# Making the low part of a weight by an accumulating DMA instead of a VectorE subtraction, in a hybrid decoder trunk on one core

## The chip, the cores and the metric

The program runs on one core of one Trainium2 chip. The metric is the device time of one execution in microseconds (us); the time of a kernel is the median of its runs.

## The reference

Two layers on x (512 tokens, width 1024, float32), then a final RMSNorm. Each layer mixes tokens, then channels:

```
h = rms_norm(x, norm1_w[l]) * (1 + sc1) + sh1
(z, xbc, dt_raw, sb_q, sb_k, sb_v, ds_q, ds_k, ds_v,
 ix_q, ix_k, ix_w, gate_logits) = split(h @ w_in[l])
y_ssd = ssd_mixer(z, xbc, dt_raw, ...)
y_sb  = stick_breaking_attention(sb_q, sb_k, sb_v)
y_dsa = dsa_attention(rope(ds_q), rope(ds_k), ds_v, rope(ix_q), rope(ix_k), ix_w)
merged = g_ssd*(y_ssd @ w_br_ssd[l]) + g_sb*(y_sb @ w_br_sb[l]) + g_dsa*(y_dsa @ w_br_dsa[l])
x = x + g1 * (merged @ w_out[l])
h2 = rms_norm(x, norm2_w[l]) * (1 + sc2) + sh2
x = x + g2 * (square(relu(h2 @ w_up[l])) @ w_down[l])
```

The sh, sc and g vectors come from `silu(c) @ ada_w[l]`; the gates are sigmoids of gate_logits. The weights are float32 and the result has to keep nearly float32 accuracy.

## The kernel before, in words

**How a float32 product is made.** TensorE is fed float32r, which keeps fewer bits than float32. Every weight W is therefore split into H, which is W rounded to float32r, and L = W - H; activations are split likewise. `mm3` (lines 222 to 225) makes one product of three matmuls: weight H by activation H (L223), weight H by activation L (L224), weight L by activation H (L225). A matmul has 512 columns, one for each token.

**Pieces of weights.** A `Job` is one 256-column group of a projection with its accumulation in PSUM. A job of 8 row blocks has two `Piece`s of 4 row blocks, 128x1024 float32 or 512 KB each; a job of 4 row blocks has one. For each piece `emit_split` (lines 509 to 536) issues the load of `raw` on SyncE's queue (L521), a cast of `raw` to `wH` on ScalarE (L533), and `wL = raw - wH` on VectorE (L534). `emit_mm` (line 538) then issues 24 matmuls for the piece: 4 row blocks, 2 groups of 128 columns, 3 matmuls each. The planner (`run`, line 580) keeps two pieces split ahead of the matmuls.

**Buffers.** `raw`, `wH` and `wL` come from pool `wp`, declared with two buffers per name. The program is built with automatic buffers, which adds more where memory allows it: a `wL` buffer is reused by the second to sixth piece after it in most places.

**Order.** `layer` (line 709) yields the jobs of the mixers in the order of the table `ORDER`; these are made by `named` (line 1491). Beside the jobs run streams: index scores, top-k by 16 rounds of max and replace on VectorE (L889, L890), stick-breaking attention (`sbatt`, with scans on VectorE at L949 and selects on GpSimd at L940), sparse attention, the SSD scan, and in layer 0 the products with `ada_w`, also on VectorE (L367). A recording layer with priorities then puts the instructions in order on each engine; splits and evacuations have high priority. Each engine works through its own list in order, and waits on semaphores.

**Other places that are spoken of.** `split` (L216, L217) makes the H and L parts of an activation on ScalarE and VectorE; the copies `paS`, `paH` and `paL` move such parts between partitions by DMA on SyncE's queue; `rope` (line 736) multiplies on GpSimd at L742; L978 makes the low part `ysbL` of the stick-breaking result; `rstd_of` (line 442) needs ScalarE's tables for logarithm and exponential, the gates (L1332) the table for tanh; L1379 is the evacuation of a `bssd` job, which needs its result.

Of the kernel before, what the change touches and what calls it, by code (L numbers as in the profile page):

```python
# [12 lines left out]
AF = mybir.ActivationFunctionType  # L13
ALU = mybir.AluOpType
# [43 lines left out]
class Piece:  # L58
# [4 lines left out]
    def __init__(self, job, k0, nk, first, last):  # L63
        self.job, self.k0, self.nk, self.first, self.last = job, k0, nk, first, last
        self.left = 0
        self.H = None
        self.keep = False
# [16 lines left out]
class Job:  # L84


    def __init__(self, name, src, nk, cols, ms, rhs, evac, need=(), kbase=0, dve=1.3, pre=None, halves=False,
                 each=False, step=4):
        self.name, self.src, self.nk, self.cols, self.ms = name, src, nk, cols, ms
        self.rhs, self.evac, self.need, self.pre = rhs, evac, need, pre  # L90
        self.kbase, self.dve, self.halves, self.each, self.step = kbase, dve, halves, each, step
        self.ps = self.fin = None
        self.bank = None
        self.open = self.left = 0

    def pieces(self):
# [78 lines left out]
def tile_trunk(ctx: ExitStack, tc: tile.TileContext, io, out, depth=DEPTH):  # L175
    nc = tc.nc
    act, dve, pool, pe, sync = nc.scalar, nc.vector, nc.gpsimd, nc.tensor, nc.sync
# [16 lines left out]
    def hl():  # L194
        return (pa.tile([P, T], F32R, name="paH", tag="pa"), pa.tile([P, T], F32R, name="paL", tag="pa"))
# [100 lines left out]
    for i, nm, src in ((0, "ada_b", io["ada_b"].rearrange("l (r c) -> (l r) c", c=P)),  # L296
# [5 lines left out]
        n = src.shape[0]  # L302
# [169 lines left out]
    def split_form(p):  # L472
        j = p.job
        src = j.form(p.k0 // 2)
        if p.keep:
            p.H, p.L = ([ap_.tile([P, T], F32R, name=n, tag=n) for _ in range(p.nk)] for n in ("aH", "aL"))
            with tc.high_priority():
                for k in range(p.nk):
                    split(src[:, k * T:(k + 1) * T], p.H[k], p.L[k])
            return  # L480
        H, L = (wp.tile([P, 1024], F32R, name=n, tag=n)[:, :p.nk * T] for n in ("wH", "wL"))
        with tc.high_priority():
            split(src, H, L)
        p.H, p.L = ([X[:, k * T:(k + 1) * T] for k in range(p.nk)] for X in (H, L))
# [24 lines left out]
    def emit_split(p):  # L509
        j = p.job  # L510
        if isinstance(j, Rows):
            split_form(p)
            return
        w = sum(n for _, n in j.cols)
        n = p.nk * w
        raw = wp.tile([P, 1024], F32, name="raw", tag="raw")
        rv = raw[:, :n].rearrange("p (k c) -> p k c", k=p.nk)
        o = 0
        k0 = j.kbase + p.k0
        for c0, m in j.cols:  # L520
            sync.dma_start(rv[:, :, o:o + m], j.src[:, k0:k0 + p.nk, c0:c0 + m])  # L521
            o += m
        if p.keep:
            w *= 2
            parts = [hl() for _ in range(0, n, w)]
        else:
            w = n
            parts = [(wp.tile([P, 1024], F32R, name="wH", tag="wH"), wp.tile([P, 1024], F32R, name="wL", tag="wL"))]
        p.H, p.L = [], []
        with tc.high_priority():  # L530
            for i, (H, L) in enumerate(parts):
                src = raw[:, i * w:(i + 1) * w]
                act.copy(H[:, :w], src)  # L533
                dve.tensor_sub(L[:, :w], src, H[:, :w])  # L534
                p.H += [H[:, k:k + n // p.nk] for k in range(0, w, n // p.nk)]
                p.L += [L[:, k:k + n // p.nk] for k in range(0, w, n // p.nk)]
# [43 lines left out]
    def run(items, ahead=2, step=2):  # L580
# [43 lines left out]
        while True:  # L624
# [38 lines left out]
            if done_k == 0:  # L663
                i = n = 0
                while len(held) < ahead:
                    look(i + 1)
                    us = [q for q in queue if isinstance(q, Unit)]
                    if i >= len(us):
                        break
                    if us[i].p.H is None:  # L670
                        emit_split(us[i].p)
                        held.append(us[i].p)
                        n += 1
                        on_dve(1.03)
                    i += 1
                if n:
                    for f in late:
                        f()
                    del late[:]
# [29 lines left out]
    def layer(l, lys):  # L709
# [781 lines left out]
        def named(n, needs=()):  # L1491
            k, i = n.rstrip("0123456789"), int(n[len(n.rstrip("0123456789")):] or 0)
            j = plain[k](i) if k in plain else kinds[k](i, needs)
            j.dve = DVE_US.get(k, j.dve)
            return j

        yield from add([named(*((n,) if isinstance(n, str) else n)) for n in ORDER if l or n != "iq1"])
        yield from pair(out_job(2), out_job(3))

# [336 lines left out]
```

## Time and profile before

| | |
|---|---|
| median of 3 runs | 1971.56 us (1969.91 to 1973.83) |
| profiled execution, its own time | 1969.26 us |
| span of its profile | 1967.5 us |
| mean granted TensorE clock | 0.997 |
| TensorE busy | 98% of the span |
| VectorE, ScalarE, GpSimd busy | 70%, 46%, 5% |
| DMA queues of SyncE, share of the 16 DMA engines | 43.2% |

Busy time of an engine is a sum over the whole span; a stage with another balance has to be looked at by itself. The mixers run from about 60 to 612 us (layer 0) and from about 1010 to 1612 us (layer 1); the MLPs fill the rest. An idle stretch before an instruction is put down to what released it last.

### The profile page before, as it was taken

To read this page: it belongs to the slowest core of one execution; us is meant where nothing else is said; L and a number is where in the kernel's file an instruction comes from. 1 tells how busy PE (TensorE), PEld (TensorE's weight loads), DVE (VectorE), ACT (ScalarE), POOL (GpSimd) and SP (SyncE) were. 2 spreads that over 40 slices of the span, in tenths; PEclk is the share of its full clock that TensorE was granted. 3 is DMA by queue.
4 is the path that set the end of the run, shared out by engine and by line. 5 is a ranking of instruction groups with operands and counts; after the bars stand their busy time and mean duration, and the time that the engine had idled before them with its cause. 6 is when DMAs were issued, how large, how long until landed. Compare 5 with 4: busy or idle time off the path is not lost.

```text
span 1967.5 us, 26644 instructions
## 1 busy us (share of the span) xinstructions
PE 1931.2 (98%) x9773; PEld 1593.6 (81%) x9773; DVE 1376.7 (70%) x2508; ACT 909.7 (46%) x1625; POOL 93.7 (5%) x135
## 2 busy tenths in 40 slices
PE   8998999999999999999999999999999999999998
PEld 5787777788888988888898787777888899888886
DVE  4899767977856986333477986687576475676874
ACT  4453626723534533242445536276335255554452
POOL 0110210100000000000000101101000000000000
PEclk9999999999999999999999999999999999999999
DMA  8764453562434695223335534324333334134051
GB/s 285 219 178 129 112 150 113 152 196 86 139 113 139 238 370 173 92 91 96 105 100 143 134 89 97 108 87 122 92 107 113 129 108 150 44 128 150 23 203 43
DMA packets 244040, 263.02 MB, mean 134 GB/s; under 512 B 34124, under 2 KB 192132, under 8 KB 243908
## 3 DMA queue, kind: packets, MB, share of 16 engines
q1 hardware_dynamic: 243328, 261.17, 43.2%
q8 instruction: 77, 1.26, 0.3%
q14 instruction: 55, 0.45, 0.1%
q10 hardware_dynamic: 356, 0.14, 0.0%
q0 software_dynamic: 224, 0.00, 0.0%
HBM read 235.43 MB, written 8.52 MB: 124 GB/s over the span
## 4 chain that ended last, share of the span: by engine, by line
PE 87%; DVE 7%; DMA 3%; issue 1%; ACT 1%; POOL 1%; SPq 0%; ACTq 0%; POOLq 0%; DVEq 0%
PE acc L223 22%; PE acc L225 22%; PE acc L224 22%; PE dn L224 3%; PE dn L225 3%; PE dn L223 3%; PE qk L249 2%; DVE wL L534 1%; PE po L1068 1%; DMA araw<-in_ada_w_dram 1%; PE tr L1059 1%; DVE sc L890 1%; DVE m L889 1%; DVE tmp L949 1%; PE po L974 1%
## 5 line engine op out<-in xcount | busy, mean ns | idle before, releaser
L223 PE MATMUL acc<-aH,wH 128*128 128x512 f32 x1544 | 613.0, 397 | 10.4 <-DVE paL L217 5.2
L225 PE MATMUL acc<-aH,wL 128*128 128x512 f32 x1544 | 606.7, 393 | 0.9 <-DVE wL L534 0.9
L224 PE MATMUL acc<-aL,wH 128*128 128x512 f32 x1544 | 606.1, 393 | 0.0
L533 ACT CAST wH<-raw 128x1024 fp32r<-128x1024 f32 (+2 forms) x262 | 266.5, 1023 | 225.9 <-PE acc L224 177.2
L223 PEld LDWEIGHTS acc<-aH,wH 128*128 128x128 f32 x1544 | 291.1, 189 | 72.4 <-DVE paL L217 6.0
L225 PEld LDWEIGHTS acc<-aH,wL 128*128 128x128 f32 x1544 | 290.9, 188 | 62.6 <-DVE wL L534 2.2
L224 PEld LDWEIGHTS acc<-aL,wH 128*128 128x128 f32 x1544 | 291.3, 189 | 57.3 <-issue 0.7
L534 DVE TENSOR_TENSOR wL<-raw,wH 128x1024 fp32r<-128x1024 f32 (+2 forms) x262 | 311.4, 1198 | 22.9 <-ACT wH L533 15.1
L367 DVE SCALAR_TENSOR_TENSOR aacc<-araw,slab,aacc 128x512 f32<-128x512 f32 x140 | 103.8, 749 | 4.5 <-DMA araw<-in_ada_w_dram 3.0
L223 PE MATMUL acc<-uH,wH 128*128 128x512 f32 x224 | 87.7, 392 | 0.0
L225 PE MATMUL acc<-uH,wL 128*128 128x512 f32 x224 | 87.2, 389 | 0.0
L224 PE MATMUL acc<-uL,wH 128*128 128x512 f32 x224 | 87.1, 389 | 0.0
L217 DVE TENSOR_TENSOR uL<-tmp,uH 128x512 fp32r<-128x512 f32 x32 | 22.0, 691 | 70.3 <-ACT uH L216 70.3
L1732 ACT ACTIVATE tmp<-acc 128x512 f32<-128x512 f32 x30 | 17.7, 594 | 111.8 <-PE acc L225 111.8
L224 PE MATMUL dn<-wL,paH 128*128 128x512 f32 x176 | 68.7, 390 | 0.1
L225 PE MATMUL dn<-wH,paL 128*128 128x512 f32 x176 | 68.5, 389 | 0.0
L223 PE MATMUL dn<-wH,paH 128*128 128x512 f32 x176 | 68.1, 389 | 0.0
L949 DVE TENSOR_TENSOR_SCAN tmp<-tmp 128x512 f32<-128x512 f32 (+1 forms) x64 | 52.5, 825 | 20.3 <-ACT tmp L942 20.3
L742 POOL TENSOR_TENSOR tmp<-tmp,slab 128x512 f32<-128x512 f32 (+1 forms) x20 | 31.6, 1578 | 722.1 <-DVE tmp L741 661.0
L1379 DVE SCALAR_TENSOR_TENSOR tmp<-tg,acc 128x512 f32<-128x512 f32 x16 | 11.0, 685 | 67.0 <-PE acc L225 67.0
L217 DVE TENSOR_TENSOR wL<-rd,wH 128x1024 fp32r<-128x1024 f32 x46 | 55.6, 1219 | 2.6 <-ACT wH L216 2.6
L216 ACT CAST wH<-rd 128x1024 fp32r<-128x1024 f32 x46 | 47.0, 1048 | 19.4 <-DVE rd L1652 14.0
(370 smaller groups left out, 3494.7 us busy)
## 6 DMA issues: line engine op xcount, KB each, us to landing
araw<-in_ada_w_dram SPq DMA_DIRECT2D x192, 256.0 KB, 5.3
raw<-in_w_in_dram SPq DMA_DIRECT2D x96, 512.0 KB, 4.0
raw<-in_w_up_dram SPq DMA_DIRECT2D x64, 512.0 KB, 4.9
raw<-in_w_down_dram SPq DMA_DIRECT2D x32, 512.0 KB, 4.7
rd<-in_w_down_dram SPq DMA_DIRECT2D x32, 512.0 KB, 7.0
raw<-in_w_in_dram SPq DMA_DIRECT2D x56, 256.0 KB, 4.3
acb<-acd SPq DMA_DIRECT2D x32, 256.0 KB, 4.7
raw<-in_w_br_ssd_dram SPq DMA_DIRECT2D x16, 512.0 KB, 4.6
```

Source lines behind the costliest of these rows:

```text
L216: act.copy(H, src)
L217: dve.tensor_sub(L, src, H)
L223: pe.matmul(ps, a[0], b[0], start=start, stop=False)
L224: pe.matmul(ps, a[0], b[1], start=False, stop=False)
L225: pe.matmul(ps, a[1], b[0], start=False, stop=stop)
L249: pe.matmul(ps, q[hh][:, cq], k[n][hh][:, ck], start=n == 0, stop=n == 1)
L367: dve.scalar_tensor_tensor(a, raw, cs[:, k:k + 1], a, op0=ALU.mult, op1=ALU.add)
L533: act.copy(H[:, :w], src)
L534: dve.tensor_sub(L[:, :w], src, H[:, :w])
L742: pool.tensor_tensor(out=b[:r], in0=b[:r], in1=sinT[:r], op=ALU.mult)
L889: dve.max(out=m8, in_=sc[tb])
L949: dve.tensor_tensor_scan(out=nv, data0=nv, data1=nv, initial=1.0, op0=ALU.mult, op1=ALU.bypass)
```

## The change

Jobs that `named` makes, which are the mixers' jobs of `ORDER`, are marked `adds`. For their pieces ScalarE makes two casts of `raw`: N = -(raw rounded), written to the buffer `wL`, and H. A DMA issued by GpSimd then adds `raw` to N in place, so that N becomes raw - H. The subtraction on VectorE is gone for these pieces. The first jobs of layer 0 (`iq0`, `misc`, `iq1`), the first pair of layer 1, the last pair of output jobs of each layer and both MLPs are made as before.

```diff
@@ class Job, __init__
+        self.adds = False
@@ emit_split
         p.H, p.L = [], []
+        if j.adds:
+            (H, N), = parts
+            with tc.high_priority():
+                act.activation(N[:, :w], raw[:, :w], AF.Copy, scale=-1.0)
+                act.copy(H[:, :w], raw[:, :w])
+                nc.gpsimd.dma_start(N[:, :w], raw[:, :w], accum_op=ALU.add)
+            p.H = [H[:, k:k + n // p.nk] for k in range(0, w, n // p.nk)]
+            p.L = [N[:, k:k + n // p.nk] for k in range(0, w, n // p.nk)]
+            return
         with tc.high_priority():
             for i, (H, L) in enumerate(parts):
@@ layer, named
             j.dve = DVE_US.get(k, j.dve)
+            j.adds = True
             return j
```

In the built program 166 pieces are changed: 166 VectorE subtractions go, 166 ScalarE instructions and 166 DMAs on GpSimd's queue come. ScalarE gets 16 table loads in place of 12. Of the 166 changed pieces, 77 take the `wL` buffer of the third piece before them, 1 that of the second, the others of the fourth or an earlier one. The line numbers after the change are one higher in the first half of `emit_split` and ten higher behind it; L535 is the cast to H, L534 the cast to N and L536 the DMA.

GpSimd's list, from the last constant it makes to the first of the index scores, where L742 (L752 after the change) is the multiplication of `rope`. Before:

```order
L274 AFFINE_SELECT slab<-slab 128x128
L732 DMA slab<-in_dt_bias_dram 16x1
L742 TENSOR_TENSOR tmp<-tmp,slab 128x512 x2
L742 TENSOR_TENSOR tmp<-tmp,slab 64x512
L742 TENSOR_TENSOR tmp<-tmp,slab 128x512 x2
L867 AFFINE_SELECT sc<-sc 128x128 x3
```

And after the change:

```order
L275 AFFINE_SELECT slab<-slab 128x128
L742 DMA slab<-in_dt_bias_dram 16x1
L752 TENSOR_TENSOR tmp<-tmp,slab 128x512
L536 DMA wL<-raw 128x1024
L752 TENSOR_TENSOR tmp<-tmp,slab 128x512
L536 DMA wL<-raw 128x1024
L752 TENSOR_TENSOR tmp<-tmp,slab 64x512
L536 DMA wL<-raw 128x1024
L752 TENSOR_TENSOR tmp<-tmp,slab 128x512 x2
L536 DMA wL<-raw 128x1024 x3
```

The first three accumulating DMAs stand between the multiplications of `rope`, one behind each.

TensorE's list with its waits, at the first piece of the first changed job, `qk0` of layer 0 (L223 to L225 before are L224 to L226 after). Before:

```order
L223 MATMUL acc<-aH,wH 128x512 [waits DVE_49]
L224 MATMUL acc<-aL,wH 128x512
L776 MATMUL tr<-slab,tmp 128x8 [waits PE_49,Activation_49]
L776 MATMUL tr<-slab,tmp 128x8 x2
L225 MATMUL pb<-aH,wL 128x512 [waits DVE_49]
L225 MATMUL pb<-aH,wL 128x512
...
L225 MATMUL acc<-aH,wL 128x512 [waits DVE_49]
```

And after the change:

```order
L226 MATMUL pb<-aH,wL 128x512
L224 MATMUL acc<-aH,wH 128x512 [waits DVE_49]
L225 MATMUL acc<-aL,wH 128x512
L224 MATMUL acc<-aH,wH 128x512 [waits DVE_49]
L225 MATMUL acc<-aL,wH 128x512
L226 MATMUL acc<-aH,wL 128x512 [waits DMASW7_49]
L226 MATMUL acc<-aH,wL 128x512
L224 MATMUL acc<-aH,wH 128x512
```

The first matmul that reads this `wL` waits for the DMA now, not for VectorE, and the rest of job `iq1` (into `pb`) stands ahead of it instead of between.

ScalarE's list with its waits at the first two changed pieces. Before:

```order
L533 CAST wH<-raw 128x1024 [waits DMAHW6_49,DMAHW7_49,DVE_49,PE_49]
L533 CAST wH<-raw 128x1024 [waits DMAHW1_49,DMAHW2_49,DVE_49,PE_49]
L765 ACTIVATE s_638<-acc,slab 16x512 [waits DMASW5_49,PE_49]
L767 ACTIVATE tmp<-acc 32x512
L745 CAST paH<-tmp 128x512 [waits DVE_49]
```

And after the change:

```order
L535 CAST wH<-raw 128x1024 [waits DMAHW6_49,DMAHW7_49,PE_49,Activation_49]
L534 ACTIVATE wL<-raw 128x1024 [waits PE_49]
L775 ACTIVATE s_638<-acc,slab 16x512 [waits DMASW5_49,PE_49]
L777 ACTIVATE tmp<-acc 32x512
L755 CAST paH<-tmp 128x512 [waits DVE_49]
L534 ACTIVATE wL<-raw 128x1024 [waits DMAHW1_49,DMAHW0_49]
L535 CAST wH<-raw 128x1024 [waits Activation_49]
```

Each piece has two ScalarE instructions now, in either order, one right behind the other.

## Rows read from the trace of the kernel before

**Rows 1.** The page, busy time by engine.
```profile
PE 1931.2 (98%) x9773; PEld 1593.6 (81%) x9773; DVE 1376.7 (70%) x2508; ACT 909.7 (46%) x1625; POOL 93.7 (5%) x135
```

**Rows 2.** Busy time by stretch: its us, engines with instructions, clock, DMA share, GB/s.
```profile
75.00:200.00 125.00, 118.34 (x557) 95.42 (x558) 121.54 (x275) 62.04 (x109) 10.11 (x19) 0.99 0.60 165
...
400.00:500.00 100.00, 100.00 (x513) 82.94 (x512) 73.08 (x108) 35.24 (x50) 0.68 (x1) 1.00 0.43 135
...
1080.00:1200.00 120.00, 115.77 (x561) 93.50 (x560) 107.69 (x246) 59.20 (x100) 14.46 (x28) 0.99 0.42 107
```

**Rows 3.** TensorE's own waits: us in total, times, longest.
```profile
PE acc L223 <- DVE paL L217: 5.2, 1, 5.2
PE qk L249 <- DMA paH<-paL: 4.5, 5, 1.9
...
PE acc L223 <- DVE ysbL L978: 4.0, 1, 4.0
...
PE acc L225 <- DVE wL L534: 0.9, 2, 0.5
```

**Rows 4.** Stretches right behind the two longest of these waits.
```profile
168.80:172.00 3.20, 3.11 (x7) 2.48 (x8) 3.20 (x9) 0.00 (x0) 0.00 (x0) 0.50 0.55 125
...
1130.70:1134.00 3.30, 3.25 (x9) 2.61 (x10) 3.30 (x5) 0.00 (x0) 0.00 (x0) 0.60 0.05 16
```

**Rows 5.** Busy time of line 534 alone, by stretch: VectorE, clock, DMA share, GB/s.
```profile
1080.00:1131.00 51.00, 7.29 (x6) 1.00 0.49 129
75.00:168.80 93.80, 14.63 (x13) 1.00 0.66 181
```

**Rows 6.** Groups of instructions by line and form: busy us, mean ns, idle before.
```profile
L534 DVE TENSOR_TENSOR wL<-raw,wH 128x1024 fp32r<-128x1024 f32 x250 | 304.7, 1228 | 22.9 <-ACT wH L533 15.1 <-issue 3.7 <-PE acc L225 3.2
...
L533 ACT CAST wH<-raw 128x1024 fp32r<-128x1024 f32 x250 | 260.5, 1047 | 225.5 <-PE acc L224 177.2 <-DMA raw<-in_w_in_dram 18.6 <-issue 6.6
```

**Rows 7.** Groups of ScalarE: a table load.
```profile
L1332 ACT ACT_TABLE_LOAD x2 | 2.6, 1283 | 0.0
```

**Rows 8.** Waits: the evacuation that needs the result of `rstd_of`.
```profile
DVE tmp L1379 <- PE acc L225: 67.0, 12, 11.9
```

**Rows 9.** DMA queue, and issues: KB each, median us from issue to landing.
```profile
q1 hardware_dynamic: 243328, 261.17, 43.2%
...
raw<-in_w_in_dram SPq DMA_DIRECT2D x96, 512.0 KB, 4.0
...
paS<-paL SPq DMA_DIRECT2D x44, 128.0 KB, 2.2
...
slab<-in_a_log_dram POOLq DMA_DIRECT2D x2, 0.1 KB, 5.2
slab<-in_dt_bias_dram POOLq DMA_DIRECT2D x2, 0.1 KB, 4.6
```

**Rows 10.** GpSimd's instructions of line 732: duration, and its DMAs' time to landing.
```profile
L732 POOL DMA_DIRECT2D slab<-in_dt_bias_dram x2: 484/493/502, 4.3 to 5.1; - x2
```

**Rows 11.** Timeline of ScalarE and GpSimd at the first two changed pieces.
```profile
51.76 1.05 ACT L533 CAST wH<-raw 128x1024 fp32r<-128x1024 f32 x1 [1.52 <-DMA raw<-in_w_in_dram]
...
55.71 1.09 POOL L742 TENSOR_TENSOR tmp<-tmp,slab 128x512 f32<-128x512 f32 x1 [50.15 <-ACT wH L533]
```

**Rows 12.** Timeline of TensorE: first use of a changed `wL`; later, matmuls around a wait.
```profile
61.11 0.62 PE L225 MATMUL acc<-aH,wL 128*128 128x512 f32 x2
...
161.41 0.39 PE L223 MATMUL acc<-aH,wH 128*128 128x512 f32 x1
161.63 0.39 PE L224 MATMUL acc<-aL,wH 128*128 128x512 f32 x1
...
168.89 0.80 PE L223 MATMUL acc<-aH,wH 128*128 128x512 f32 x1 [5.21 <-DVE paL L217]
...
170.33 0.63 PE L223 MATMUL acc<-aH,wH 128*128 128x512 f32 x1
170.76 0.63 PE L224 MATMUL acc<-aL,wH 128*128 128x512 f32 x1
```

**Rows 13.** Busy time by stretch early in layer 0's mixers; columns as in rows 2.
```profile
80.00:100.00 20.00, 20.00 (x98) 16.09 (x97) 17.56 (x41) 10.21 (x22) 0.36 (x1) 1.00 0.84 224
100.00:120.00 20.00, 19.90 (x94) 16.14 (x93) 20.00 (x47) 13.88 (x24) 4.07 (x6) 1.00 0.74 208
```

## The prediction

> **What bounds the kernel now.** I read the busy shares first: TensorE is busy 98% of the span, VectorE 70% [rows 1]. So whatever VectorE is spared can be worth no more than the stretches in which TensorE stands still for it. Next, the same by stretch: from 75 to 200 us VectorE is busy 121.5 of 125 us, from 1080 to 1200 us 107.7 of 120 us, and TensorE shows its gaps there; in a plain stretch such as 400 to 500 us VectorE has 27 us to spare and TensorE has no gap [rows 2]. Last, whom TensorE waits for: 5.2 us once for a low part that VectorE made late (layer 0, until 168.9 us) and 4.0 us once for `ysbL` (layer 1, until 1130.7 us). For the weights' own subtraction it waits 0.9 us in all [rows 3]. The subtractions hurt, then, by the place that they take in VectorE's list in two full stretches, and not by their own latency.
>
> A wait costs more than itself. Before the first, matmuls start 0.22 us apart; behind it 0.43 us [rows 12]. The granted clock is 0.50 for 3.2 us behind the first wait and 0.60 for 3.3 us behind the second [rows 4], the lower of the two levels for most of that time; that loses 1.6 and 1.3 us more.
>
> **The change, part by part.**
>
> *Subtractions removed.* 166 by 1.23 us [rows 6] are 204 us of VectorE. On the path lie only those ahead of the two waits: 14.6 us (13 instructions) from 75 to 168.8 us and 7.3 us (6) from 1080 to 1131 us [rows 5]. Both are more than VectorE was late, 5.2 and 4.0 us, so I take both waits away with their slow clock: 5.2 + 1.6 + 4.0 + 1.3 = 12.1 us gained. At worst VectorE's place is taken by another late engine and half remains: 6.
>
> *Casts added.* 166 by 1.05 us [rows 6] are 174 us more on ScalarE, whose share goes from 46% to about 55%. Its waits say how early casts stand: 177 us of them are for TensorE to release a buffer [rows 6], so it had finished its part long before and has that time to give. Four more table loads are 4 by 1.28 = 5.1 us [rows 7]; they stand at the logarithm and exponential of the SSD norm, whose consumer waits 67 us for TensorE anyway [rows 8]. Both cost nothing while that cover holds; without it the table loads would cost up to 5.1 us.
>
> *The DMA's latency.* No row shows an accumulating DMA. Call L its time from issue to landing. The queue of SyncE moved 261 MB in 43.2% of 1967.5 us, or 307 GB/s, so 512 KB take 1.7 us of transfer. Lower end: a 128 KB copy lands in 2.2 us, and 384 KB more at that rate make 3.5 us. Upper end: the slowest small load that GpSimd issued took 5.2 us; with the bytes counted twice, because source and destination are both read, 5.2 + 3.4 = 8.6 us. The nearest row is a small load of GpSimd's own queue, 4.6 us, and with the bytes once I take L = 4.6 + 1.7 = 6.3 us [rows 9].
>
> For the fixed part the row says 4.6 to 5.2 us on GpSimd's queue [rows 9]. The Trainium skill (DMA: Bandwidth & Descriptors, "Anatomy of one DMA — SWDGE (gpsimd) path") gives 2.0 us and the bytes at 436 GB/s, an estimate of 3.2 us here, and the trace's small loads do not agree. By the page the sum would be some 2 us lower, since the first piece below would not wait; I stay with the rows.
>
> *Does L reach TensorE?* A piece is 24 matmuls by 0.227 us = 5.4 us. Where `wL` is the buffer of the third piece before, it comes free when that piece's last matmul ends, and two whole pieces, 10.9 us, run before the new one is needed. In this time ScalarE makes both casts (2.1 us) and the DMA lands: 2.1 + 6.3 = 8.4 us, at the upper end 10.7 us. Hidden by both, but by 0.2 us only at the upper end. That holds for the 77 tightest pieces in a plain stretch; the others have a piece or more in hand, or attention work between. Cost 0.
>
> *The first piece of layer 0.* Nothing is ahead of it. Its DMA stands behind a `rope` multiplication that ends at 55.71 + 1.09 = 56.8 us; the raw weight's cast was at 51.76 us, so N is ready [rows 11]. The DMA lands at 56.8 + 6.3 = 63.1 us, and its matmul ran at 61.1 us [rows 12]: 2.0 us lost (0 at the lower L, 4.3 at the upper). The second and third piece need theirs 5.4 us later each and fit.
>
> *GpSimd's issue.* 166 by about 0.5 us [rows 10] are 83 us on an engine that is 5% busy [rows 1]. What queues behind an issue that waits for its cast are the attention's selects and `rope`, which wait for ScalarE themselves. Nothing, but for the first piece.
>
> *DMA traffic.* 87 MB more in 537 + 602 us of mixers raise the share from some 0.4 to 0.55, or 0.8 if bytes count twice. Who stands on it: TensorE waits 4.5 us for copies between partitions [rows 3]. I let these grow by a third, 1.5 us (0 to 4.5, a doubling). The loads of `raw` run several pieces ahead.
>
> **Sum:** -12.1 + 2.0 + 1.5 = -8.6 us. Against the profiled execution's own 1969.26 us that is 1960.7; the runs' median stands 2.3 us above that execution, so the same -8.6 on the median gives **1963.0 us**. The forecast's own range is 1957 to 1967.6. A measurement here tells 0.2%, about 4 us, from no change: faster is below 1967.6, slower above 1975.5.
>
> **The rivals.**
>
> *ScalarE takes VectorE's place: no change.* Its casts now come in pairs, so an evacuation that falls behind them waits 1.05 us more, and the low part that TensorE missed at 168.9 us starts with a ScalarE cast. For it: VectorE's part is only half of that chain. Against: ScalarE is busy 62 of 125 us in that stretch [rows 2]. Then 6 us are gained and 3.5 to 8.8 lost: -2.5 to +2.8, 1969 to 1974 us.
>
> *The DMA is slower than the buffers: slower.* Beyond L = 8.8 us the ring of three buffers sets the pace: 5.4 + 2.1 + L for three pieces in place of 16.3. It is felt in plain stretches, some 38 of the 77 pieces. At L = 9.5 it costs 0.23 us by 38, about what is gained, and there the sign turns. At L = 10 it is 0.4 by 38 = 15 us, 1978 us; at 12, 40 us, 2003; at 14, 66 us and more, 2030 to 2050. For it: no row shows the operation, and the upper end passes by 0.2 us. Against: nothing in this trace moves 512 KB that slowly.
>
> *The DMA engines fill up early in layer 0: slower.* The share is 0.84 from 80 to 100 us and 0.74 from 100 to 120 us [rows 13]. Three pieces in each 20 us, at twice 1.7 us, add 0.51, which makes 1.35 and 1.25: 12 us of work too much in 40 us, of which the loads in flight get their part. Layer 0 then loses 12 us and its gain of 6.8, layer 1 keeps 5.3 and 3.5 are paid: 1971.6 + 12 - 5.3 + 3.5 = 1982 us. If bytes count once, the shares stay at 1.1 and 1.0 and it fades. The Trainium skill (DMA: Bandwidth & Descriptors, "Issuing engines are not separate DMA queues") says that DMAs of all issuers run on the same 16 engines and interleave, and Collectives: The Full Stack ("The bandwidth ceiling") that an add needs two source reads and halves the rate; no run here shows the second.
>
> That the change doesn't do what it says is excluded: the built program has the 166 DMAs.
>
> **How the numbers follow.** Forecast 0.45; no change 0.20; slow DMA 0.25, since its price is unmeasured and the margin thin; full DMA engines 0.10. So faster 0.45, same 0.20, slower 0.35. The likeliest case gives 1963. The range goes from 1957, where the first piece and the copies cost nothing and small waits go too, up to 2010, a DMA of about 12 us; left out are a slower one (0.12) and a larger gain (0.05).
>
> **What would show it.** Right: VectorE's line 534 group has 166 fewer; from 75 to 200 us VectorE is near 101 of 125 us; the waits for `paL` and `ysbL` are gone and with them the stretches at half clock; the new DMA's median landing is 5 to 8.6 us; TensorE waits for it once, at about 61 us. Wrong: landings above 9 us and a row of waits of the L226 matmuls for the DMA through the plain stretches, or DMA shares near 1 from 80 to 120 us with casts waiting for `raw`, or the same two waits with ScalarE's casts as their cause.

## The result and the profile after

The changed kernel takes 2029.76 us (median of 4 runs, 2027.95 to 2033.39), the kernel before 1971.97 us beside it: a ratio of 1.0298, interval 1.0286 to 1.0311. The profiled execution took 2030.06 us, its span is 2028.1 us.

First the busy shares on the page of the changed kernel, as in [rows 1]:

```profile
PE 1949.6 (96%) x9773; PEld 1605.0 (79%) x9773; DVE 1202.6 (59%) x2342; ACT 1068.6 (53%) x1795; POOL 221.5 (11%) x301
```

VectorE has its 166 instructions and 174 us less, ScalarE 159 us more (the forecast reckoned 204 and 179). TensorE is busy 18 us longer with the same 9773 matmuls: some ran at the lower clock. Next the stretches of [rows 2] and [rows 13], in the same columns:

```profile
75.00:200.00 125.00, 109.59 (x489) 87.55 (x488) 103.22 (x259) 70.13 (x115) 19.69 (x34) 0.91 0.92 226
400.00:500.00 100.00, 94.44 (x481) 77.02 (x481) 58.56 (x102) 52.76 (x82) 16.84 (x20) 1.00 0.93 236
1080.00:1200.00 120.00, 106.58 (x499) 86.28 (x498) 96.16 (x244) 70.79 (x114) 23.87 (x37) 0.96 0.78 176
80.00:100.00 20.00, 17.37 (x80) 13.88 (x79) 13.79 (x37) 10.88 (x23) 1.88 (x3) 0.91 0.92 211
100.00:120.00 20.00, 19.64 (x90) 15.60 (x90) 19.57 (x55) 12.48 (x21) 3.16 (x5) 1.00 0.91 232
```

VectorE is indeed relieved, 103.2 us in place of 121.5 from 75 to 200 us, and yet TensorE works less there: 489 matmuls against 557. The column that jumped is the second from the right: the DMA engines' share is 0.92 where it was 0.60, and 0.93 in the plain stretch from 400 to 500 us where it was 0.43. The granted clock is 0.91 in the first stretch. Then whom TensorE waits for, as in [rows 3]:

```profile
PE tr L797 <- DMA tmp<-in_k_sel_dram: 11.7, 2, 8.3
PE acc L224 <- DVE paL L218: 11.1, 2, 8.5
PE qk L250 <- DMA paH<-paL: 10.4, 4, 4.8
PE acc L226 <- DMA wL<-raw: 5.3, 2, 2.9
...
PE acc L224 <- DVE ysbL L988: 3.5, 1, 3.5
...
PE qk L250 <- DMA paH<-paH: 3.0, 1, 3.0
```

The two waits that should have gone are still there (11.1 and 3.5 us), and waits for DMAs have come, above all for transfers that the change did not add: an 8 KB constant `k_sel`, the 128 KB copies. Summed over all rows of this view, TensorE waits 70.1 us against 27.8 before; 37.3 of it for DMAs against 9.7. The other 18 us of the span's 60.6 are the slower matmuls behind these waits. The DMA queues, then issues with their KB and median us to landing, as in [rows 9]:

```profile
q1 hardware_dynamic: 243328, 261.17, 41.9%
q0 software_dynamic: 24128, 87.04, 23.0%
...
wL<-raw POOLq DMA_DIRECT2D x166, 512.0 KB, 6.3
...
raw<-in_w_in_dram SPq DMA_DIRECT2D x96, 512.0 KB, 5.3
...
paS<-paL SPq DMA_DIRECT2D x44, 128.0 KB, 3.9
```

and of the DMA's own line (L536) its time to landing:

```profile
DMA to landing us min/median/max: 4.5/6.3/10.6
```

The accumulating DMA lands in the 6.3 us that the forecast took for it. What grew is everything else on the DMA engines: the load of `raw` from 4.0 to 5.3 us, the copy `paS` from 2.2 to 3.9 us. GpSimd's queue takes 23.0% of the engines for 87 MB, SyncE's 41.9% for 261 MB: by the byte 1.65 times as much. One of the 166 DMAs is 0.230 by 2028.1 / 166 = 2.8 us of all 16 engines.

### The profile page after: what moved, and what is told of

It reads as the page before. It is cut to its first block, busy times and chain, and to the rows that moved or that the text cites. A ratio compares the mean times of both kernels' runs of the same rounds, so it can differ in the third digit from the quotient of the medians.

```text
span 2028.1 us, 27155 instructions
## 1 busy us (share of the span) xinstructions
PE 1949.6 (96%) x9773; PEld 1605.0 (79%) x9773; DVE 1202.6 (59%) x2342; ACT 1068.6 (53%) x1795; POOL 221.5 (11%) x301
## 3 DMA queue, kind: packets, MB, share of 16 engines
q1 hardware_dynamic: 243328, 261.17, 41.9%
## 5 line engine op out<-in xcount | busy, mean ns | idle before, releaser
L224 PE MATMUL acc<-aH,wH 128*128 128x512 f32 x1544 | 618.5, 401 | 16.4 <-DVE paL L218 11.1
L226 PE MATMUL acc<-aH,wL 128*128 128x512 f32 x1544 | 608.5, 395 | 5.6 <-DMA wL<-raw 5.3
L225 PE MATMUL acc<-aL,wH 128*128 128x512 f32 x1544 | 610.3, 395 | 0.0
L224 PEld LDWEIGHTS acc<-aH,wH 128*128 128x128 f32 x1544 | 293.4, 190 | 79.5 <-DVE paL L218 12.5
L226 PEld LDWEIGHTS acc<-aH,wL 128*128 128x128 f32 x1544 | 293.5, 190 | 70.0 <-DMA wL<-raw 6.5
L225 PEld LDWEIGHTS acc<-aL,wH 128*128 128x128 f32 x1544 | 293.9, 190 | 58.1 <-issue 0.6
L536 POOL DMA_DIRECT2D wL<-raw x166 | 143.2, 863 | 1149.9 <-ACT wL L534 687.5
L535 ACT CAST wH<-raw 128x1024 fp32r<-128x1024 f32 x166 | 173.2, 1044 | 173.4 <-PE acc L225 80.6
L534 ACT ACTIVATE wL<-raw 128x1024 fp32r<-128x1024 f32 x166 | 175.4, 1057 | 21.3 <-PE acc L226 17.7
L544 DVE TENSOR_TENSOR wL<-raw,wH 128x1024 fp32r<-128x1024 f32 (+2 forms) x96 | 108.5, 1141 | 93.1 <-ACT wH L543 92.8
L543 ACT CAST wH<-raw 128x1024 fp32r<-128x1024 f32 (+2 forms) x96 | 93.0, 982 | 60.7 <-PE acc L225 54.2
L224 PE MATMUL acc<-uH,wH 128*128 128x512 f32 x224 | 87.7, 392 | 0.0
L226 PE MATMUL acc<-uH,wL 128*128 128x512 f32 x224 | 87.2, 389 | 0.0
L225 PE MATMUL acc<-uL,wH 128*128 128x512 f32 x224 | 87.1, 389 | 0.0
L224 PE MATMUL dn<-wH,paH 128*128 128x512 f32 x176 | 68.5, 389 | 0.0
L225 PE MATMUL dn<-wL,paH 128*128 128x512 f32 x176 | 68.5, 389 | 0.0
L226 PE MATMUL dn<-wH,paL 128*128 128x512 f32 x176 | 68.5, 389 | 0.0
```

Source lines behind the costliest of these rows:

```text
L224: pe.matmul(ps, a[0], b[0], start=start, stop=False)
L225: pe.matmul(ps, a[0], b[1], start=False, stop=False)
L226: pe.matmul(ps, a[1], b[0], start=False, stop=stop)
L534: act.activation(N[:, :w], raw[:, :w], AF.Copy, scale=-1.0)
L535: act.copy(H[:, :w], raw[:, :w])
L536: nc.gpsimd.dma_start(N[:, :w], raw[:, :w], accum_op=ALU.add)
```

## The experiments

Theories: **TRAFFIC**, the bytes fill the DMA engines; **HOLD**, `raw` stays taken until the DMA lands; **QUEUE**, GpSimd's list stands at issues that wait; **CASTS**, ScalarE's second cast. And for the gain that did not come: **REFILL** or **LIST ORDER** against **CAPACITY**. In the runs with spare tiles line numbers are one to six higher than after the change, in those with `paL` moved up to three.

### The change without its DMA, and with a tiny one

```diff
-                nc.gpsimd.dma_start(N[:, :w], raw[:, :w], accum_op=ALU.add)
```

> The change without its DMA: ScalarE makes both casts, nothing is added to N, so the low part is -H and the third product has other values (left out: the addition). Theory TRAFFIC (the 166 DMAs fill the 16 DMA engines, the loads and the copies between partitions land late): VectorE and ScalarE work as in the changed kernel but the bytes are gone, so the two waits for paL and ysbL go and the time is near 1960 us (1955 to 1968). Theory HOLD (raw and wL stay taken until the DMA lands, so SyncE's list stands at its raw loads and what is behind them comes late): also near 1960. Theory QUEUE (GpSimd's selects and rope multiplications stand behind DMA issues that wait for casts): also near 1960. Theory CASTS (174 us more on ScalarE, its evacuations come late): 2000 us or more, since nothing of ScalarE's work is taken away.

```diff
-                nc.gpsimd.dma_start(N[:, :w], raw[:, :w], accum_op=ALU.add)
+                nc.gpsimd.dma_start(N[:, :8], raw[:, :8], accum_op=ALU.add)
```

> The change with a DMA that adds 8 of 1024 columns, 4 KB in place of 512 KB: GpSimd's list has the same issues with the same waits, and the order on the engines is nearly that of the changed kernel (left out: the addition on the other 1016 columns). TRAFFIC: the DMA share falls from 0.85 to about 0.45 in layer 0's mixers, small copies land in 2.2 us again, time 1960 to 1972 us. HOLD: the small DMA still takes 4 to 5 us from issue to landing in place of 6.3, so raw and wL are held nearly as long and two thirds of the loss stay: 2000 to 2020 us. QUEUE: the issues and waits stay, 2015 to 2030 us. CASTS: 2015 to 2030 us.

Measured: 1977.03 us (ratio 1.0026, 1.0011 to 1.0040) without, 1973.76 us (1.0013, 1.0000 to 1.0027) with the tiny one. So 56 of the 58 us go with the bytes; the tiny DMA lands in 2.0 us at the median, though, and not in the 4 to 5 that its expectation took, so it holds `raw` for a short time only and is no test of HOLD. GpSimd's list with all its issues and waits costs nothing by itself, and QUEUE and CASTS fall as main causes. But none of the theories had the gain right: no run reached 1960. With the tiny addition VectorE is as free as forecast, 97.6 of 125 us (columns as above):

```profile
75.00:200.00 125.00, 115.07 (x545) 93.66 (x545) 97.55 (x247) 74.14 (x116) 21.31 (x35) 0.97 0.62 162
```

and TensorE waits longer than before for the same tile:

```profile
PE acc L224 <- DVE paL L218: 8.0, 1, 8.0
```

The timeline of that run, ScalarE and VectorE, shows where `paL` was (start, duration, engine, line):

```profile
157.93 0.59 ACT L217 CAST paH<-acc 128x512 fp32r<-128x512 f32 x1 [2.98 <-PE acc L226]
...
162.16 0.68 DVE L900 MATCH_REPLACE8 sc<-m,sc 128x512 f32<-128x512 f32 x1
162.87 0.69 DVE L899 MAX8 m<-sc 128x8 f32<-128x512 f32 x1
...
165.90 0.69 DVE L899 MAX8 m<-sc 128x8 f32<-128x512 f32 x1
...
166.71 0.68 DVE L900 MATCH_REPLACE8 sc<-m,sc 128x512 f32<-128x512 f32 x1
167.30 0.68 DVE L218 TENSOR_TENSOR paL<-acc,paH 128x512 fp32r<-128x512 f32 x1
```

`paH` is done at 158.5 us, `paL` starts at 167.3: 8.8 us later, in which VectorE, never idle, works mostly through top-k rounds (some 6 us). In the kernel before the distance was 6.0 us (ScalarE's cast at 161.6 us), one subtraction among it; in the changed kernel it is 9.6 us (`paH` done at 176.4, `paL` started at 185.9). The room that the subtractions left was filled by top-k, whose last round of layer 0 starts at 182.1 us in place of 200.1; VectorE's list was no shorter in front of `paL`.

### The second cast alone

```diff
-                nc.gpsimd.dma_start(N[:, :w], raw[:, :w], accum_op=ALU.add)
+                dve.tensor_add(N[:, :w], raw[:, :w], N[:, :w])
```

> ScalarE makes both casts and VectorE adds raw to N in place (the same result, no DMA): the kernel before with one cast more for each of 166 pieces. TRAFFIC, HOLD and QUEUE: near the kernel before, 1968 to 1980 us, a little above it for the chain of two casts ahead of VectorE. CASTS: 2010 us or more, since VectorE has its old load too.

Measured: 1976.05 us, 1.0023 (1.0014 to 1.0033). A cast more for each piece costs 5 us; the forecast had it free. TensorE waits 3.9 us for ScalarE's `at` (L975) and 2.0 us for an evacuation (`mg`, L1342) in that run; in the kernel before it was none and 0.2 us. Other waits shrank, so the sum over all rows, 29.2 us, is hardly above the 27.8 before; TensorE is busy 5.7 us longer at a lower mean clock (0.994 against 0.997).

### The traffic alone, and as plain copies

```diff
-                act.activation(N[:, :w], raw[:, :w], AF.Copy, scale=-1.0)
                 act.copy(H[:, :w], raw[:, :w])
-                nc.gpsimd.dma_start(N[:, :w], raw[:, :w], accum_op=ALU.add)
+                dve.tensor_sub(N[:, :w], raw[:, :w], H[:, :w])
+                nc.gpsimd.dma_start(spare[next(turn) % 2][:, :w], H[:, :w], accum_op=ALU.add)
```

The lines that make the two spare tiles and the counter `turn` are not shown, here and in the other runs with spare tiles.

> The splits of the kernel before (cast on ScalarE, subtraction on VectorE), and beside them an accumulating DMA of GpSimd from wH to one of two spare tiles that nobody reads: the traffic of the change alone, without its second cast and without holding raw or wL. wH is held by TensorE for longer than that DMA takes. TRAFFIC: the DMA share is as in the changed kernel (0.8 to 1.0 in layer 0), copies between partitions land in some 4 us in place of 2.2, and the time is above that of the changed kernel or near it, since VectorE is not relieved: 2010 to 2050 us. HOLD: 1970 to 1985 us. QUEUE: 2000 us or more, with waits for selects and rope multiplications. CASTS: 1970 to 1980 us.

Measured: 2007.18 us, 1.0180 (1.0162 to 1.0199). The same bytes, read from `wH` and written where nobody looks, cost 36 us. The expectation's 2010 to 2050 was a little high: traffic is the largest part, but not all. Queue, issues and two waits of that run:

```profile
q0 software_dynamic: 24128, 87.04, 23.4%
...
paS<-paL SPq DMA_DIRECT2D x44, 128.0 KB, 4.3
```

```profile
PE qk L251 <- DMA paH<-paL: 12.5, 2, 7.1
PE tr L803 <- DMA tmp<-in_k_sel_dram: 11.3, 2, 7.5
```

It is the changed kernel's picture: copies land in twice their time, and TensorE waits for copies and for `k_sel`. Then the same DMAs without the addition:

```diff
-                nc.gpsimd.dma_start(spare[next(turn) % 2][:, :w], H[:, :w], accum_op=ALU.add)
+                nc.gpsimd.dma_start(spare[next(turn) % 2][:, :w], H[:, :w])
```

> The run with the traffic alone, its 166 DMAs as plain copies from wH to the spare tiles in place of additions: the same 87 MB written, issued by the same engine at the same places. If the price is that of an addition (source and destination both read: 23.4% of the DMA engines for 87 MB against 43.1% for SyncE's 261 MB), the share of GpSimd's queue falls to about 14 to 15% and the time to 1980 to 1992 us. If any transfer of this size costs it (bytes written, or the 4 KB rows inside SBUF): 2000 to 2010 us as with additions.

Measured: 1982.68 us, 1.0055 (1.0041 to 1.0070), inside the first case. The queue's row:

```profile
q0 software_dynamic: 24128, 87.04, 13.5%
```

A plain copy of 512 KB is 0.135 by 1983.3 / 166 = 1.6 us of all engines, an adding one 2.8 us: 1.7 times. And 1.7 times the share costs three times as much, 36 us against 11.

### Half the bytes

```diff
+            m2 = w // 2
...
+                act.activation(N[:, :m2], raw[:, :m2], AF.Copy, scale=-1.0)
                 act.copy(H[:, :w], raw[:, :w])
+                nc.gpsimd.dma_start(N[:, :m2], raw[:, :m2], accum_op=ALU.add)
+                dve.tensor_sub(N[:, m2:w], raw[:, m2:w], H[:, m2:w])
```

> The change for half of each piece's columns: the DMA adds 256 KB, VectorE subtracts the other 512 columns (the same result). TRAFFIC in proportion to bytes: half of the loss, 1995 to 2005 us, the DMA's landing near 4.5 us. TRAFFIC as a queue that hurts when the DMA engines come near full (0.97 and 1.00 from 50 to 150 us in the changed kernel): far less than half, 1975 to 1988 us. HOLD alone: the landing falls by a third, 2005 to 2015 us.

Measured: 1989.34 us, 1.0094 (1.0076 to 1.0112), between two of the cases: 18 of 58 us, a third for half the bytes (VectorE keeps half of each subtraction here). The loss grows faster than the bytes, as between plain and adding copies.

### The source: HBM in place of `raw`

```diff
-                nc.gpsimd.dma_start(N[:, :w], raw[:, :w], accum_op=ALU.add)
+                nv = N[:, :n].rearrange("p (k c) -> p k c", k=p.nk)
+                o = 0
+                for c0, m in j.cols:
+                    nc.gpsimd.dma_start(nv[:, :, o:o + m], j.src[:, k0:k0 + p.nk, c0:c0 + m], accum_op=ALU.add)
+                    o += m
```

> The changed kernel, but the accumulating DMA reads the weights from HBM a second time and not from raw (same bytes added, same result, 1 to 4 DMAs for a piece): raw is free again after the two casts, as early as ScalarE is done. TRAFFIC (the runs so far: bytes alone cost 36 us beside the kernel before, and without them the change costs 3 to 6): nothing is spared, 2020 to 2045 us. HOLD: SyncE's loads run ahead again and most of the 17 us that traffic (36) and casts (5) leave of the 58 go: 2000 to 2015 us.

Measured: 2039.84 us, 1.0346 (1.0330 to 1.0362). This was no clean test of HOLD: read from HBM, the same bytes took 29.9% of the DMA engines in place of 23.0%, and the 512 KB additions landed in 7.9 to 12.3 us (the median for each weight tensor). What freeing `raw` gave cannot be told from what the longer transfers took.

### Casts and traffic, with `raw` free and with `raw` held

```diff
-                nc.gpsimd.dma_start(N[:, :w], raw[:, :w], accum_op=ALU.add)
+                nc.gpsimd.dma_start(spare[next(turn) % 2][:, :w], H[:, :w], accum_op=ALU.add)
```

> Both casts on ScalarE, no subtraction, and the accumulating DMA goes from wH to a spare tile that nobody reads (left out: the addition to N, so the low part is -H): traffic and casts, without raw held and without a wait for the landing. If the parts add up: 1971 + 36 + 5 = 2012 us, and what is missing to 2030 is holding or waiting. If casts and traffic make each other worse: 2022 to 2032 us.

```diff
-                nc.gpsimd.dma_start(spare[next(turn) % 2][:, :w], H[:, :w], accum_op=ALU.add)
+                nc.gpsimd.dma_start(spare[next(turn) % 2][:, :w], raw[:, :w], accum_op=ALU.add)
```

> The run before it with raw in the place of wH as the source of the DMA, so that raw stays taken until it lands; still nobody waits for the spare tile (left out: the addition to N). HOLD: 10 us or more above the run with wH as the source. WAIT FOR wL: the same time as with wH as the source within 3 us, and the rest up to the changed kernel's 2030 is the wait for the landing of wL.

Measured: 2003.93 us (1.0169, 1.0153 to 1.0185) with `wH` as the source, 2026.64 us (1.0279, 1.0261 to 1.0296) with `raw`. The first is 8 us under the sum of the parts (VectorE is relieved here, and was not where the traffic stood alone). The second is 23 us above it for one changed word, as HOLD expected. But its trace does not show HOLD's mechanism. If `raw` came free late and its next load with it, ScalarE's casts would wait longer for that load. With `wH` as the source they waited (us, times, longest):

```profile
ACT wH L541 <- DMA raw<-in_w_in_dram: 8.1, 3, 4.1
ACT wL L540 <- DMA raw<-in_w_in_dram: 7.7, 2, 5.1
```

and with `raw`, less:

```profile
ACT wL L540 <- DMA raw<-in_w_in_dram: 6.0, 2, 3.1
ACT wH L541 <- DMA raw<-in_w_in_dram: 4.0, 2, 2.2
```

TensorE's own waits for DMAs are not longer either, 17.3 us against 22.6. SyncE's list now waits for the DMA at the loads of `raw`, in the second run and in the changed kernel:

```profile
SPq L528 <- DMA spare<-raw: 103.2, 26, 12.4
```

```profile
SPq L522 <- DMA wL<-raw: 553.0, 96, 17.9
```

In the kernel before it waited there for the subtraction, 721.8 us in 138 times, so a standing list is nothing new. And the changed kernel stands there for the DMA five times as long as the second run, yet takes only 3 us more, less than the spread of the runs. So neither the hold nor the wait for the landing of `wL` can be read off as a price. With `raw` as the source the DMA also no longer waits for a cast: GpSimd's issues waited 103 times for a load of `raw` (`raw<-in_w_in_dram`), where they had waited 133 times for the cast to H, so the additions run at other times; and the order of the instructions differs a little between the two programs. Which of these makes the 23 us, and through which reader they reach TensorE, the runs don't tell.

### The late constant on another queue

```diff
-            sync.dma_start(selT, io["k_sel"])
+            act.dma_start(selT, io["k_sel"])
```

> The changed kernel with one word changed: the 8 KB load of k_sel, for which TensorE waited 3.4 and 8.3 us, is issued by ScalarE and not behind SyncE's loads and copies. If it came late because SyncE's list stood (at copies that wait, and at raw loads whose buffers the accumulating DMA holds): both waits go with their slow clock, 2012 to 2020 us. If it came late because the DMA engines were full: it lands as late, 2026 to 2034 us. If TensorE then only waits for the next late transfer (a copy paH): 2024 us or more, with longer waits for those.

Measured: 2027.72 us, 1.0284 (1.0270 to 1.0299): nothing gained. Of 11.7 us of waits for `k_sel` 3.8 were left, but TensorE then waited 7.8 us for a `tmp` of the stick-breaking attention (L962) and 5.0 us for a product of `ada` (`aacc`), for which it had not waited. With so much late, taking away one wait uncovers the next.

### `paL` out of VectorE's list

```diff
-                split(ps, H, L)
+                t = tmp()
+                act.copy(H, ps)
+                act.copy(t, ps)
+                pool.tensor_tensor(out=L, in0=t, in1=H, op=ALU.subtract)
                 sbt[key[i]] = (stack, twice)[i](H, L)
```

In the kernel before:

> The kernel before, subtractions on VectorE and all, with one edit elsewhere: the low parts paL of the stick-breaking queries and keys (16 of them) are made by GpSimd from a copy in SBUF that ScalarE makes, and leave VectorE's list. Theory LIST ORDER (the wait for paL comes from 4 to 9 us of top-k rounds and scans that stand ahead of it in VectorE's list, and the planner refills with them what the subtractions leave): the wait of 5.2 us and its slow clock go, 1960 to 1967 us, although VectorE keeps 204 us of subtractions. Theory CAPACITY (VectorE is full from 75 to 200 us, whatever stands where): 16 subtractions of 0.7 us are 11 of some 1200 us, the next low part is late instead, 1969 to 1973 us.

Measured: 1977.23 us, 1.0036 (1.0024 to 1.0048), slower than either theory had it. The wait for `paL` went, but TensorE now waits for the next reader of the same list:

```profile
PE acc L225 <- DVE wL L534: 10.1, 5, 3.8
```

So LIST ORDER alone falls, and CAPACITY's "the next low part is late instead" is what happened. VectorE is some microseconds behind whatever stands where, and the first tile that TensorE needs from it shows that: two of these waits, 5.4 us, fall in layer 0's full stretch, the longest in layer 1's. Both had to go together, which the change without its DMA, with the same edit, does:

> The change without its DMA (left out: the addition, so the low part is -H) and with the 16 paL made by GpSimd from a copy that ScalarE makes. The run without the DMA alone stood at 1977 us with 8.2 us of waits for paL. REFILL: these and their slow clock of some 3 us go, 1962 to 1969 us. CAPACITY: VectorE was relieved already, nothing changes, 1974 to 1979 us. If casts are the price (ScalarE 174 us more, and 16 more copies): 1978 to 1985 us.

Measured: 1968.48 us, 0.9981 (0.9971 to 0.9991), 8.5 us under the run without that edit; REFILL had 1962 to 1969. TensorE waits for no `paL` of VectorE and no `wL` of these pieces, and of the two old waits this is left:

```profile
PE acc L224 <- DVE ysbL L991: 2.2, 1, 2.2
```

So VectorE's relief does pay (8.7 us against the run with `paL` aside and all subtractions), once nothing that TensorE needs soon stands behind the work that moves up. But with the second cast paid it is 2.5 us against the kernel before, and in this arrangement that is an upper end: the bytes come on top.

### The change for 28 pieces alone

```diff
-            j.adds = True
+            j.adds = 2 <= st.setdefault("njob", 0) <= 8
+            st["njob"] += 1
```

and `paL` on GpSimd as above.

> The change for the third to ninth job of each layer's mixers alone, 28 pieces in place of 166, with the 16 paL made by GpSimd (the same result). The traffic is 28 of 166, some 6 us by proportion and less where the DMA engines have room; the run with paL aside alone lost 10 us on wL subtractions that stood late in VectorE's list, and those pieces now have none. REFILL with paL out of the list: the 5.2 and 4.0 us of waits go, 1962 to 1969 us. If the traffic counts most where these pieces stand (DMA share 0.84 from 80 to 100 us in the kernel before): 1972 to 1980 us.

Measured: 1991.04 us, 1.0099 (1.0084 to 1.0114), outside both cases, and 14 us above the run with `paL` aside alone (1977.23). A sixth of the DMAs costs a quarter of the change's loss, because they stand in the crowded stretch, where they come late themselves:

```profile
PE acc L226 <- DMA wL<-raw: 14.0, 8, 4.4
```

```profile
100.00:150.00 50.00, 44.83 (x201) 36.19 (x199) 48.34 (x122) 34.45 (x57) 13.86 (x20) 0.93 0.93 228
```

The share of the DMA engines is 0.93 from 100 to 150 us, where it was 0.65 in the kernel before. Just where VectorE is full and relief would pay, the DMA engines have no room. No version that computes the whole result ran below the kernel before.

### The subtraction on GpSimd

```diff
-                act.activation(N[:, :w], raw[:, :w], AF.Copy, scale=-1.0)
                 act.copy(H[:, :w], raw[:, :w])
-                nc.gpsimd.dma_start(N[:, :w], raw[:, :w], accum_op=ALU.add)
+                pool.tensor_tensor(out=N[:, :w], in0=raw[:, :w], in1=H[:, :w], op=ALU.subtract)
```

> The 166 low parts by a subtraction on GpSimd (same result; one cast on ScalarE as before, no DMA): VectorE is relieved of 204 us as in the change, without the change's traffic and casts. Theory REFILL (the planner puts top-k rounds into the room that the subtractions leave, and paL stays 5 to 9 us behind them in VectorE's list): TensorE still waits 5 to 9 us for paL, time 1968 to 1977 us. Theory CAPACITY (VectorE full from 75 to 200 us is what holds TensorE up): the waits for paL and ysbL go, 1958 to 1964 us. Theory SHARED (elementwise work on GpSimd and on VectorE slow each other): the scans and top-k of VectorE last longer than 1.22 and 0.55 us, 1980 us or more.

And with the 16 `paL` on GpSimd as well:

> The low parts of the weights and the 16 paL on GpSimd (same result): of what TensorE waited for in layer 0's full stretch nothing is left in VectorE's list. REFILL: now the list's backlog meets no reader of paL or wL, and the 5.2 us of the kernel before and their slow clock go, perhaps the 4.0 us for ysbL stay: 1958 to 1968 us, under both kernels. CAPACITY: the same 1958 to 1964 us, and no better than the run with wL alone on GpSimd. SHARED, or GpSimd's own list too long (a piece is some 2.6 us on it, and a paL behind it waits): 1975 us or more.

Measured: 2045.99 us (1.0372, 1.0356 to 1.0387) and 2043.52 us (1.0368, 1.0353 to 1.0383): SHARED in both. Three groups of VectorE in the first run, by line and form (busy us, mean ns, idle before):

```profile
L368 DVE SCALAR_TENSOR_TENSOR aacc<-araw,slab,aacc 128x512 f32<-128x512 f32 x140 | 125.7, 906 | 5.3 <-DMA araw<-in_ada_w_dram 2.6 <-ACT aacc L366 1.0
...
L753 DVE TENSOR_TENSOR tmp<-tmp 128x512 f32<-128x512 f32 x18 | 25.5, 1420 | 10.2 <-POOL tmp L752 10.2
...
L899 DVE MAX8 m<-sc 128x8 f32<-128x512 f32 x32 | 21.9, 685 | 0.4
```

and in the kernel before:

```profile
L367 DVE SCALAR_TENSOR_TENSOR aacc<-araw,slab,aacc 128x512 f32<-128x512 f32 x140 | 103.8, 749 | 4.5 <-DMA araw<-in_ada_w_dram 3.0
...
L743 DVE TENSOR_TENSOR tmp<-tmp 128x512 f32<-128x512 f32 x18 | 12.6, 697 | 14.7 <-POOL tmp L742 14.7
...
L889 DVE MAX8 m<-sc 128x8 f32<-128x512 f32 x32 | 22.1, 690 | 0.6
```

The addition of two tiles takes 1420 ns in place of 697 while GpSimd subtracts beside it (2517 ns a piece); MAX8, with one tile to read, is unchanged. VectorE lost 204 us of work and stayed full: 120.0 of 125 us from 75 to 200 us.

## Why the prediction was wrong

It said 1963.0 us with 1957 to 2010; 2029.76 was measured. The runs give the 58 us in steps, each the difference of two medians: the change without its DMA stands 6 us above the kernel before, the traffic brings it 27 us further (1977.03 to 2003.93), `raw` as the DMA's source 23 (to 2026.64), and 3 are left (to 2029.76), within the spread of the runs. The order of the instructions differs between these programs too, so a step of a few us is not exact: the run with the tiny DMA, which has both casts as well, stands 3 us above the kernel before and not 6.

**The gain, -12.1 us: failed at "Both are more than VectorE was late ... so I take both waits away".** VectorE's time in the stretch was forecast well (near 101 us from 75 to 200, measured 103.2). But a list of instructions does not move up when some of them go: top-k rounds moved into the room, and with the DMA or its bytes taken away TensorE waited 8.2 or 8.0 us for `paL` in place of 5.2. Comparing sums of busy time with lateness was the wrong measure; what counts is what stands between ScalarE's cast and `paL` in VectorE's list, and that could be read from the order of the changed program before any run.

**"DMA traffic", +1.5 us (0 to 4.5): failed, the largest error.** Copies were to grow by a third; 2.2 us became 3.9. The bound of 4.5, a doubling of the waits for copies, left out that other small transfers, which TensorE had never waited for, would come late too: `k_sel` alone took 11.7 us. Of the forecast's share of 0.55 or 0.8 the second came true, 0.83 from 60 to 612 us and 0.72 from 1010 to 1612, but by luck: 87 MB at the forecast's own 307 GB/s are 284 us of all engines, 0.25 of its 1139 us of mixers, so its sum should have given some 0.65, or 0.9 with the bytes twice. And no cost was worked out from the share. The rival "the DMA engines fill up early in layer 0" had the mechanism, with a chance of 0.10; it failed in price, 1982 us, because it reckoned only the work that does not fit in 40 us, and not the delay of everything else on the engines from 0.9 on, nor layer 1. Its sign came true: shares of 0.92 and 0.91 from 80 to 120 us, where casts waited 12.8 us for `raw` and had waited for none before. The range ended at 2010, for a DMA of about 12 us, though the slow DMA's own list makes 2003 of that.

**The DMA's source: missing from the sum.** "The loads of `raw` run several pieces ahead" was taken as cover without asking what releases `raw`. Before, it was VectorE's subtraction, which lasts 1.2 us; now it is the DMA's landing, 6.3 us after its issue. Reading `raw` in place of `wH` costs 23 us; that the late release is the reason is not shown, and the cause of these 23 us stays open.

**Casts, 0 us: 5 us measured.** "Both cost nothing while that cover holds" failed: in the run with the second cast alone TensorE met new waits for ScalarE (3.9 and 2.0 us) and a lower clock. The group of the cast to H in the changed kernel:

```profile
L535 ACT CAST wH<-raw 128x1024 fp32r<-128x1024 f32 x166 | 173.2, 1044 | 173.4 <-PE acc L225 80.6 <-DMA raw<-in_w_in_dram 41.5 <-issue 24.6
```

The cover itself was mostly left. Ahead of all casts of [rows 6] ScalarE waited 177 us for TensorE; now it is 81 ahead of this group, 18 ahead of the casts to N and 54 ahead of the pieces made as before, 153 in all. A large sum of waits did not mean that no single result of ScalarE comes late. The 41.5 us of waits for `raw` are no sure sign of a held `raw`: where the DMA leaves it free they were 43.1 us with the traffic alone and 8.1 with casts and traffic.

**What was right.** L: 6.3 us median, as taken, though by two errors that cancel (see the last section). That it hardly reaches TensorE: 5.3 us in two waits, where one was forecast, of 2.0 us; that one measured 2.4, at 62 us. The rival of the slow DMA against the ring of three buffers did not come about, as the median stayed under its 8.8 us. GpSimd's issues cost nothing by themselves.

One of those two waits shows how the three queues hang together. The timeline of the changed kernel, ScalarE, GpSimd and TensorE:

```profile
415.90 1.05 ACT L534 ACTIVATE wL<-raw 128x1024 fp32r<-128x1024 f32 x1
...
418.41 0.67 POOL L1263 TENSOR_SCALAR_AFFINE_SELECT acb<-acb 128x512 f32<-128x512 f32 x1 [2.97 <-DMA acb<-acd]
419.03 0.86 POOL L536 DMA_DIRECT2D wL<-raw  x1
...
427.07 0.50 PE L226 MATMUL acc<-aH,wL 128*128 128x512 f32 x1 [2.88 <-DMA wL<-raw]
```

N is ready at 417.0 us. The DMA is issued 2 us later, behind a select that waited for a late load of the SSD; it lands 8 us after that, and TensorE has stood for 2.9 us. So the tile that the wait names, `wL<-raw`, is late in part because another transfer was.

## What to carry to other kernels

Moving work from an engine to a DMA spends a shared resource: price it as time of the DMA engines, an addition at 1.7 times a copy, against the share in the stretch where it will run, and expect everything on those engines to come late before the share reaches 1 (with half the bytes it was 0.78 from 75 to 200 us, and the copy `paS` took 3.0 us in place of 2.2). What the DMA reads matters as well, 23 us here, for a reason that these runs leave open. And before counting on relief of an engine, look in its list for what stands ahead of the tile that is waited for: if other work moves up into the room, nothing is gained.

## What the runs showed that was not expected

The price of an addition: 2.8 us of all 16 DMA engines for 512 KB against 1.6 us for a plain copy. The Trainium skill (Collectives: The Full Stack, "The bandwidth ceiling: the fold count and why AG ≠ RS ≠ AR") says of the reduce step of a collective that its add needs two source reads, which halves the rate; the runs show 1.7 times the engines' time, not quite 2. The forecast took 1.7 us of transfer; by that rule of the Trainium skill it would be twice that, an estimate of 3.4 us, and nearer.

The fixed part of a GpSimd DMA: the addition of 4 KB landed in 2.0 us at the median, where the forecast had taken 4.6 us from small loads out of HBM. The Trainium skill (DMA: Bandwidth & Descriptors, "Anatomy of one DMA — SWDGE (gpsimd) path") gives 2.0 us, and that run agrees; the 6.3 us were met because a fixed part taken too long made up for a transfer taken too short.

VectorE doubled in time beside GpSimd: 697 to 1420 ns for an addition of two tiles in SBUF, no change for MAX8. The Trainium skill (SBUF — State Buffer, "Who interferes with whom") says that an instruction of VectorE with two inputs in SBUF contends with one of GpSimd that reads SBUF, and that one with at most one such input, outside the two-port modes, does not; these rows agree.
